# A decoder trunk: the order of its projections, its split buffers and the products of its recurrence

## The chip, the cores and the metric

The kernel runs on one core of one Trainium2 chip, as one program. The metric is the device time of one execution in microseconds (us). A profile of one execution stands beside it: it lists for each engine when it worked. PE (TensorE) multiplies matrices, PEld is its weight load, DVE (VectorE) and ACT (ScalarE) work element by element, POOL (GpSimd) does small and strided work, and SP (SyncE) issues most of the transfers. Each engine works through its own queue of instructions in order.

## The reference, cut to what matters

256 tokens of 2048 features pass through one layer of a hybrid decoder. The weights are read once, and all of it is float32.

```
h  = RMSNorm(x)
c, b, xa, za, q, f, iv, og, ga, gb = split(h @ W_in)
yA = b * conv3(c * xa) * silu(za)
o  = gated recurrence over the tokens: queries silu(q), keys (1-lb)*sigmoid(-f),
     values iv, decay lb + (1-lb)*sigmoid(f) per token and feature, 8 heads of 128
yB = RMSNorm per head(o) * silu(og)
x  = x + (sigmoid(ga) * (yA @ W_a) + sigmoid(gb) * (yB @ W_b)) @ W_o
x  = x + sigmoid(RMSNorm(x) @ W_pg) * (p @ W_pp)
out = RMSNorm(x)
```

The last but one line matters for the first two parts of the change: p @ W_pp (called PP here; p has only 256 features) depends on nothing before it, while RMSNorm(x) @ W_pg (called PG, the gate) needs all that comes before.

The recurrence matters for the third. For a pair of tokens s <= t of one head, its matrix is a[s, t] = sum over k of key[s, k] * query[t, k] * exp(B[t, k] - B[s, k]), where B is the running sum of the logarithm of the decay. A product of matrices can only be formed if the exponential is split into one factor for s and one for t, and for numbers that don't overflow both have to be taken from a reference token between s and t. So the matrix is cut by levels: at level B, the tokens are in blocks of B, and pairs that lie in the two halves of the same block take the middle of the block as reference. What is left (blocks of 2) is corrected by one factor per pair.

## The kernel before, in words

**Streaming.** The weights arrive as chunks of 256 rows by 512 columns. `load` (L94) issues the transfers into three raw buffers of two chunks each. `split` (L108) writes each chunk as a high part in fp32r on ScalarE (`whi`, L118) and the rest on VectorE (`wlo`, L119), into one of four pairs of buffers, or of six "late" pairs near the end. `product` (L844) multiplies it: three fp32r matmuls of 128x512 (L847 to L849) for each of two feature blocks and each of two halves of the tokens, so twelve a chunk. The other operands are split in the same way by `put` (`xh` at L196 on ScalarE, `xl` at L197 on VectorE).

**The order of groups.** A group is 512 columns of one weight matrix, in all its chunks (eight, four for W_a and W_b, one for W_pp). The list `groups` (L124) sets the order: the fields of W_in in two rounds (f, q, iv, og, c, xa, za, b, with j = 0 and then 1), then ga, gb, A and B four times, then O four times, then PP0, PG0, PP1, PG1, PP2, PG2, PP3, PG3. Splits run three chunks ahead of the products (`ahead`, L840). Around the last group they run up to five further ahead. A group fills two PSUM banks of the four with the tag "g"; four more with the tag "s" serve the recurrence.

**Epilogues.** What becomes of a finished group is a generator (`ep_f`, `ep_q`, ..., `ep_pp` at L646, `ep_pg` at L653). The main loop advances each active one by a step per chunk, and the step's instructions are ordered behind that chunk's split on ScalarE and VectorE. The compiler's scheduler may move matmuls of independent groups past each other on TensorE. `ep_pp` copies the two banks of PP to SBUF (L649); `ep_pg` takes the sigmoid from the banks of PG (L659), multiplies, adds to x and squares. `ep_o` adds to x, and then brings the result into the layout with features on the partitions by way of DRAM (`turned`, L223: four writes, a read, and a transposition at L238), and `put` makes x1's operands of it, which PG needs.

**The recurrence.** `hgrn` (L350) runs once for each half of the heads (j = 0, 1), as part of the epilogue of og. It has six levels (LEVELS, L31: 128, 64, 32, 16, 8, 4). For each, `level` (L402) subtracts the reference (L413 on VectorE, L414 on POOL) and takes exponentials on ScalarE (L415, L416); `combine` (L387) multiplies them with keys and queries, two quarters on VectorE and two on POOL (L396); `products` (L364) forms a full 128x128 matrix for each of four heads (L368); `keep` (L371) copies those entries that a mask names. A further burst of the same size is the block of the second 128 tokens against the first. Then the pairs of 2 are corrected by a factor and its reciprocal (L457 to L468), and one burst of eight products of 128x128 (L477) gives the diagonal blocks. The finished matrices meet the values at L488 to L490.

**Start and end.** The first transfers are x and the first chunk of f (L147 to L167, L723); eight bf16 matmuls without use keep TensorE busy until they land (L734). The last group is worked in three parts (L920), so that the end of the work behind it (`last_half`, L673, and `last_norm`, L688) is short.

The loop that issues all of this, with `steps` a flat list of (group, chunk):

```
for pos, (gi, c) in enumerate(steps[:last_group]):
    while done < min(pos + 1 + ahead(pos), len(steps)):
        split(done)
        done += 1
    product(psum[t], ...)
    advance()
    if c == nch - 1:
        active.append(epilogues[kind](j, psum))
        step(active[-1])
```

Of the kernel before, what the change touches and what calls it, by code (L numbers as in the profile page):

```python
# [15 lines left out]
P = 128  # L16
T = 256
# [13 lines left out]
LEVELS = [128, 64, 32, 16, 8, 4]  # L31
# [13 lines left out]
def hybrid_kernel(ctx, tc, xT, x, pT, prm, gfin, masks, w_in, w_a, w_b, w_o, w_pg, w_pp, out):  # L45
# [47 lines left out]

    def load(pos):  # L94
        w, g, c = stream[pos]
        nch = w.shape[2]
        key = (id(w), g, c // 2)
        if key not in loaded:
            raw = wp.tile([P, 2, 2 * CW], F32, tag="raw", bufs=3, name=nm("raw"))
            loaded[key] = raw  # L100
            if nch == 1 or FIRST <= pos < FIRST + 4:
                for i in range(min(nch, 2)):
                    nc.sync.dma_start(out=raw[:, i, :], in_=w[g, :, c + i, :])
            elif pos >= FIRST:
                nc.sync.dma_start(out=raw, in_=w[g, :, c : c + 2, :])
        return loaded[key]

    def split(pos, halves=(0, 1)):  # L108
        w, g, c = stream[pos]
        src = load(pos)[:, c % 2, :]  # L110
        pool, n = (pools["late"], 6) if pos >= last_group + 2 else (wp, 4)
# [12 lines left out]
    groups = []  # L124
# [15 lines left out]
    last_group = len(steps) - w_pg.shape[2]  # L140

    LEAD, AHEAD = 3, 4
    TOKENS, NORM = 6, 10
    FIRST = 6


    prm_t = const.tile([P, PRM_N], F32, name="prm_t")  # L147
    xraw = [t4() for _ in range(4)]
# [6 lines left out]
    def load_first(c, eng):  # L155

        raw, w = load(c)[:, c % 2, :], stream[c][0][0, :, c, :]
        for s in (slice(0, CW), slice(CW, 2 * CW)):
            eng.dma_start(out=raw[:, s], in_=w[:, s])


    load_first(0, nc.scalar)
    nc.sync.dma_start(out=prm_t, in_=prm)
    load_x(0, 1)
    load_x(1, 1)
    load_x(2, 2)
    load_first(1, nc.sync)  # L167
# [9 lines left out]
    carry = const.tile([P, 1024], F32, name="carry")  # L177
    nc.gpsimd.memset(carry, 1.0)
    nc.gpsimd.memset(carry.rearrange("p (n c) -> p n c", c=SCAN)[:, :, 0:1], 0.0)
    mask_t = const.tile([P, len(LEVELS) + 4, P], mybir.dt.int32, name="mask_t")  # L180
# [98 lines left out]
    def ep_f(j, psum):  # L279
# [16 lines left out]
        for h in range(4):  # L296
# [21 lines left out]
        nc.vector.tensor_tensor_scan(  # L318
            out=b, data0=carry, data1=lf, initial=0.0, op0=ALU.mult, op1=ALU.add
        )  # L320
# [29 lines left out]
    def hgrn(j):  # L350

# [8 lines left out]
        both = tmp.tile([P, 4, P], F32, tag="both", bufs=1, name=nm("both"))  # L360
        nc.gpsimd.memset(both, 0.0)
        aoff = tmp.tile([P, 4, P], F32, tag="aoff", bufs=1, name=nm("aoff"))

        def products(X):  # L364
            bk = bank("s")
            for h in range(4):
                s = slice(h * P, (h + 1) * P)
                nc.tensor.matmul(bk[:, s], X[:, 0, h, :], X[:, 1, h, :], start=True, stop=True)  # L368
            return bk

        def keep(dst, mask, src):  # L371
            nc.vector.copy_predicated(
                out=dst, mask=mask_t[:, mask : mask + 1, :].to_broadcast([P, 4, P]), data=src
            )
# [12 lines left out]
        def combine(e, B):  # L387

            X = t4("X", 2).rearrange("p (w h t) -> p w h t", w=2, h=4)
            ev, kv, qv = tiles(e, B), tiles(kT, B), tiles(qT, B)  # L390
            xv = X.rearrange("p w h (n two c) -> p w h n two c", two=2, c=B // 2)
            for w, blk, half, src, eng in (
                (0, 0, 0, kv, nc.vector), (0, 1, 1, kv, nc.gpsimd),
                (1, 1, 0, qv, nc.vector), (1, 0, 1, qv, nc.gpsimd),
            ):
                eng.tensor_tensor(  # L396
                    out=xv[:, w, :, :, half, :], in0=ev[:, :, blk, :, half, :], in1=src[:, :, blk, :, half, :],
                    op=ALU.mult,
                )
            return X  # L400

        def level(B):  # L402

            n, h = 1024 // B, B // 2
# [3 lines left out]
            if B > SCAN:  # L408
                nc.scalar.activation(out=el, in_=halves(y, B)[0], func=AF.Exp, scale=-1.0)
                nc.scalar.activation(out=er, in_=br, func=AF.Exp)  # L410
            else:
                ref = bl[:, :, h - 1 : h].to_broadcast([P, n, h])
                nc.vector.tensor_tensor(out=el, in0=bl, in1=ref, op=ALU.subtract)  # L413
# [3 lines left out]
            return combine(e, B)  # L417


# [6 lines left out]
        X = level(LEVELS[0])  # L426
        yield
        yield
        for i in range(len(LEVELS)):
            nxt = level(LEVELS[i + 1]) if i + 1 < len(LEVELS) else None  # L430
            bk = products(X)
            yield
            yield
            keep(both, i, heads(bk))
            yield
            X = nxt

# [9 lines left out]
        X = t4("X", 2).rearrange("p (w h t) -> p w h t", w=2, h=4)  # L447
        ev, kv, qv = (z.rearrange("p (h k t) -> p h k t", h=4, k=2) for z in (e, kT, qT))
        nc.vector.tensor_tensor(out=X[:, 0], in0=ev[:, :, 0], in1=kv[:, :, 0], op=ALU.mult)
        nc.gpsimd.tensor_tensor(out=X[:, 1], in0=ev[:, :, 1], in1=qv[:, :, 1], op=ALU.mult)  # L450

        f, rf = (t4()[:, :512] for _ in range(2))
        bl, br = halves(b, 2)
        nc.vector.tensor_tensor(
            out=f.rearrange("p (n c) -> p n c", c=1), in0=br, in1=bl, op=ALU.subtract
        )
        nc.scalar.activation(out=f, in_=f, func=AF.Exp)  # L457
        nc.vector.reciprocal(out=rf[:, :256], in_=f[:, :256])
        yield
        nc.vector.reciprocal(out=rf[:, 256:], in_=f[:, 256:])  # L460
        yield
        bo = products(X)
        k2, q2 = tiles(kT, 2), tiles(qT, 2)
        fv, rv = (z.rearrange("p (h k n) -> p h k n", h=4, k=2) for z in (f, rf))
        for blk in range(2):
            kk, qq = k2[:, :, blk, :, 1 - blk, 0], q2[:, :, blk, :, 1 - blk, 0]
            nc.vector.tensor_tensor(out=kk, in0=kk, in1=rv[:, :, blk], op=ALU.mult)
            nc.gpsimd.tensor_tensor(out=qq, in0=qq, in1=fv[:, :, blk], op=ALU.mult)  # L468
            keep(a[:, blk], len(LEVELS) + blk, both)
        yield  # L470
        nc.vector.tensor_copy(out=aoff.rearrange("p h t -> p (h t)"), in_=bo)
        yield
        bk = [bank("s") for _ in range(2)]
        for blk in range(2):
            for h in range(4):
                s = slice(h * T + blk * P, h * T + (blk + 1) * P)
                nc.tensor.matmul(  # L477
                    bk[blk][:, h * P : (h + 1) * P], kT[:, s], qT[:, s], start=True, stop=True
                )
        yield  # L480
        yield
        for blk in range(2):
            keep(a[:, blk], len(LEVELS) + 2 + blk, heads(bk[blk]))
        yield
        o = [bank("s") for _ in range(2)]
        for h in range(4):
# [5 lines left out]
            )  # L492
        yield
# [152 lines left out]
    def ep_pp(j, psum):  # L646
        pw = t4("pw", 2)
        for t in range(NT):
            nc.scalar.activation(out=pw[:, t * CW : (t + 1) * CW], in_=psum[t], func=AF.Copy)  # L649
        state["pw", j] = pw  # L650
        yield

# [360 lines left out]
```

## Time and profile before

| | |
|---|---|
| median of 3 runs | 842.39 us (842.17 to 842.98) |
| span of the profiled execution | 840.7 us, 9809 instructions |
| its own time beside the span | none is given; the runs are 1.5 to 2.3 us longer than the span |
| busy, of the span | PE 98%, DVE 63%, ACT 52%, POOL 11% |
| read from HBM, written | 170.82 MB, 11.53 MB, 217 GB/s over the span |

How to read what is quoted of the profile: a line of the time line has the start in us, the duration in us, the engine, the line of the kernel (L847), the operation, the tile that is written and those that are read (buffer numbers left out), and the shapes. "x4" means four of them in a row. "[3.67 <-ACT t L659]" means that the engine was idle for 3.67 us before, and that the instruction of L659 on ScalarE released it. A line of the groups has the busy time in us and the mean of one in ns, and behind the second bar the idle time before them with its releasers. A line of the chain has the start, the time on the chain, and what it was. Matmuls overlap: one is given as 0.39 us long, but the next one starts after less than that, so their price is the distance between starts. An fp32 product appears as two matmul records, an fp32r product as one.

### The profile page before, as it was taken

Reading aid. Unit: us, or ns where it says so; the run is one execution under the profiler, and the core shown is the slowest. Engines: PE = TensorE matmul, PEld = TensorE weight load, DVE = VectorE, ACT = ScalarE, POOL = GpSimd, SP = SyncE. Lnnn points to the kernel's source line nnn. Section 1 sums busy time; section 2 is a strip of 40 time slices with the busy share of each in tenths; the row PEclk is TensorE's granted clock in tenths of the full one; section 3 lists DMA queues with packets and bytes.
Section 4 is the critical chain, followed back from the end, with each engine's and each line's share of the span. In section 5 each row is a group of like instructions: output and inputs, shape, how many; then the busy total and the mean of one; then the engine's idle time right before and its main releaser. Section 6 shows DMA issues by size and latency. Waiting matters only on the chain.

```text
span 840.7 us, 9809 instructions
## 1 busy us (share of the span) xinstructions
PE 824.8 (98%) x3752; PEld 684.8 (81%) x3752; DVE 528.3 (63%) x600; ACT 435.9 (52%) x563; POOL 91.6 (11%) x76
## 2 busy tenths in 40 slices
PE   8999999999999999999999999999999999999985
PEld 6888888888888888888888888888888888878865
DVE  6557687777674777877546446455555666655552
ACT  7565654545564654545544444444444555654543
POOL 1000054100000243100001001001001000002110
PEclk9999999999999999999999999999999999999998
DMA  9976555648775555458557557556556877864522
GB/s 327 375 257 242 186 198 172 229 151 267 267 236 189 193 196 187 168 190 285 186 195 244 200 200 232 195 189 232 203 200 220 288 262 259 306 229 175 201 76 101
DMA packets 40080, 183.01 MB, mean 218 GB/s; under 512 B 4576, under 2 KB 14048, under 8 KB 22112
## 3 DMA queue, kind: packets, MB, share of 16 engines
q1 hardware_dynamic: 39456, 181.33, 62.2%
q10 hardware_dynamic: 576, 1.05, 0.4%
q8 instruction: 29, 0.48, 0.2%
q14 instruction: 19, 0.16, 0.1%
HBM read 170.82 MB, written 11.53 MB: 217 GB/s over the span
## 4 chain that ended last, share of the span: by engine, by line
PE 95%; DMA 2%; issue 1%; ACT 1%; DVE 1%; POOLq 0%; POOL 0%; SPq 0%; ACTq 0%
PE g L847 31%; PE g L849 31%; PE g L848 31%; PE s L368 1%; DMA raw<-in_w_pg 1%; DVE wlo L119 1%; ACT whi L118 1%; PE s L477 0%; DMA t<-in_xT 0%; PE s L490 0%; PE s L489 0%; PE s L488 0%; ACT xs L700 0%; ACT t L683 0%; DVE t L679 0%
## 5 line engine op out<-in xcount | busy, mean ns | idle before, releaser
L119 DVE TENSOR_TENSOR wlo<-raw,whi 128x1024 fp32r<-128x1024 f32 (+1 forms) x294 | 360.3, 1229 | 273.5 <-ACT whi L118 273.0
L118 ACT ACTIVATE whi<-raw 128x1024 fp32r<-128x1024 f32 (+1 forms) x294 | 309.0, 1053 | 353.4 <-PE g L849 316.1
L847 PE MATMUL g<-whi,xh 128*128 128x512 f32 (+1 forms) x912 | 353.6, 389 | 6.0 <-ACT t L659 3.7
L848 PE MATMUL g<-wlo,xh 128*128 128x512 f32 (+1 forms) x912 | 353.1, 387 | 0.0
L849 PE MATMUL g<-whi,xl 128*128 128x512 f32 (+1 forms) x912 | 352.6, 387 | 0.1
L847 PEld LDWEIGHTS g<-whi,xh 128*128 128x128 f32 x912 | 172.2, 189 | 41.6 <-ACT t L659 4.1
L849 PEld LDWEIGHTS g<-whi,xl 128*128 128x128 f32 x912 | 172.1, 189 | 35.1 <-DVE xl L197 0.5
L848 PEld LDWEIGHTS g<-wlo,xh 128*128 128x128 f32 x912 | 172.0, 189 | 34.3 <-DVE wlo L119 0.5
L848 PE MATMUL g<-wlo,mh 128*128 128x512 f32 x128 | 49.6, 389 | 0.0
L849 PE MATMUL g<-whi,ml 128*128 128x512 f32 x128 | 49.5, 389 | 0.0
L847 PE MATMUL g<-whi,mh 128*128 128x512 f32 x128 | 49.5, 389 | 0.0
L613 POOL TENSOR_TENSOR t<-ga,gb 128x512 f32<-128x512 f32 x8 | 14.1, 1791 | 249.1 <-DVE gb L609 249.1
L849 PEld LDWEIGHTS g<-whi,ml 128*128 128x128 f32 x128 | 24.0, 188 | 5.0
L848 PEld LDWEIGHTS g<-wlo,mh 128*128 128x128 f32 x128 | 24.0, 188 | 5.0
L847 PEld LDWEIGHTS g<-whi,mh 128*128 128x128 f32 x128 | 24.0, 188 | 4.9
L414 POOL TENSOR_TENSOR t<-b 128x512 f32<-128x512 f32 x10 | 20.9, 2086 | 65.3 <-DMA raw<-in_w_in 33.6
L396 POOL TENSOR_TENSOR X<-t,kT 128x256 f32<-128x256 f32 x12 | 14.1, 1174 | 99.4 <-ACT t L410 57.7
L847 PE MATMUL g<-whi,yaTh 128*128 128x512 f32 x64 | 24.9, 389 | 0.0
L848 PE MATMUL g<-wlo,yaTh 128*128 128x512 f32 x64 | 24.9, 389 | 0.0
L849 PE MATMUL g<-whi,yaTl 128*128 128x512 f32 x64 | 24.9, 389 | 0.0
L847 PE MATMUL g<-whi,ybTh 128*128 128x512 f32 x64 | 24.9, 389 | 0.0
L848 PE MATMUL g<-wlo,ybTh 128*128 128x512 f32 x64 | 24.9, 389 | 0.0
(148 smaller groups left out, 556.1 us busy)
## 6 DMA issues: line engine op xcount, KB each, us to landing
raw<-in_w_in SPq DMA_DIRECT2D x91, 1024.0 KB, 4.9
raw<-in_w_o SPq DMA_DIRECT2D x16, 1024.0 KB, 5.4
raw<-in_w_pg SPq DMA_DIRECT2D x16, 1024.0 KB, 4.8
turn<-t SPq DMA_DIRECT2D x72, 128.0 KB, 2.9
t<-turn SPq DMA_DIRECT2D x18, 512.0 KB, 5.1
raw<-in_w_a SPq DMA_DIRECT2D x8, 1024.0 KB, 5.0
raw<-in_w_b SPq DMA_DIRECT2D x8, 1024.0 KB, 5.0
raw<-in_w_in SPq DMA_DIRECT2D x8, 512.0 KB, 7.8
```

The lines of the kernel that those rows point to most:

```text
L118: a = nc.scalar.activation(out=hi[:, s], in_=src[:, s], func=AF.Copy)
L119: v = nc.vector.tensor_tensor(out=lo[:, s], in0=src[:, s], in1=hi[:, s].bitcast(F32), op=ALU.subtract)
L368: nc.tensor.matmul(bk[:, s], X[:, 0, h, :], X[:, 1, h, :], start=True, stop=True)
L396: eng.tensor_tensor(out=xv[:, w, :, :, half, :], in0=ev[:, :, blk, :, half, :], in1=src[:, :, blk, :, half, :], op=ALU.mult,)
L414: nc.gpsimd.tensor_tensor(out=er, in0=br, in1=ref, op=ALU.subtract)
L613: nc.gpsimd.tensor_tensor(out=spread(m, t), in0=blocks(ga[:, s]), in1=blocks(gb[:, s]), op=ALU.add)
L847: nc.tensor.matmul(psum, oh, hi, start=first, stop=False)
L848: nc.tensor.matmul(psum, oh, lo, start=False, stop=False)
L849: nc.tensor.matmul(psum, ol, hi, start=False, stop=last)
```

## The change

Three things are changed together.

1. **PP first.** The four PP groups move to the front of the list, ahead of f. p's two feature blocks and the chunks of W_pp are the first transfers. `ep_pp` copies each result to SBUF (one bank on ScalarE, one on VectorE, some chunks later) and writes it to a DRAM buffer, 512 KB for each; `load_pw` reads it back when the gate's group starts. PP2 and PP3 use the banks with the tag "s". O is followed by PG0, PG1, PG2, PG3 directly.
2. **Ten pairs for the gate.** From the gate's first chunk on (`gate`), four of ten chunks go to the four pairs of before and six to the "late" pairs, so that ten pairs serve all the gate's groups. `ahead` grows by one for every four chunks.
3. **The recurrence in blocks of 32.** The levels 32, 16, 8 and 4 only have entries inside the diagonal blocks of 32x32. For each head, level and block there is now one product of 32 rows by 32 columns (over all 128 features), whose place among the columns of TensorE is given by `tile_position`; the 64 of a half come as one burst. A second burst has the 32x32 blocks of level 64 (16), those of the final diagonal (32), the 64x64 blocks of level 128 (8) and the four full products of the second 128 tokens against the first. Masks shrink to 32 columns. The multiplies of `combine` are all on VectorE, the reference is subtracted from the whole tile on VectorE, and the reciprocal becomes exp(-x) with one Newton step. The scan over 1024 columns becomes four of 256.

The core of the diff (new lines have new numbers; L706 of the changed file is the copy of a PP bank on ScalarE, L901 to L903 are its large products):

```diff
-LEVELS = [128, 64, 32, 16, 8, 4]
+LEVELS = [32, 16, 8, 4]
+NARROW, Q = len(LEVELS), 32
...
+        pool, n = (pools["late"], 6) if pos >= gate and (pos - gate) % 10 >= 4 else (wp, 4)
...
+    groups = [("PP", j, w_pp, j, "pT") for j in range(4)]
...
-    for j in range(4):
-        groups.append(("PP", j, w_pp, j, "pT"))
-        groups.append(("PG", j, w_pg, j, "x1T"))
+    groups += [("PG", j, w_pg, j, "x1T") for j in range(4)]
...
+    gate = len(steps) - 4 * w_pg.shape[2]
...
+    load_half(0, 0, nc.scalar)
+    for k in range(2):
+        nc.sync.dma_start(out=praw[:, k * T : (k + 1) * T], in_=pT[:, k, :])
+    load_half(0, 1, nc.scalar)
+    for i in range(2):
+        load_half(1, i, nc.sync)
     nc.sync.dma_start(out=prm_t, in_=prm)
-    load_x(0, 1)
-    load_x(1, 1)
-    load_x(2, 2)
-    load_first(1, nc.sync)
+    for c in (2, 3):
+        for i in range(2):
+            load_half(c, i, nc.sync)
+    for c in (0, 1):
+        for i in range(2):
+            load_half(FIRST + c, i, nc.sync)
+        load_x(2 * c, 2)
+    load_x(4, 2)
+    load_x(6, 2)
...
-                ref = bl[:, :, h - 1 : h].to_broadcast([P, n, h])
-                nc.vector.tensor_tensor(out=el, in0=bl, in1=ref, op=ALU.subtract)
-                nc.gpsimd.tensor_tensor(out=er, in0=br, in1=ref, op=ALU.subtract)
+                n, h = 1024 // B, B // 2
+                ref = bl[:, :, h - 1 : h].to_broadcast([P, n, B])
+                nc.vector.tensor_tensor(
+                    out=e.rearrange("p (n c) -> p n c", c=B), in0=b.rearrange("p (n c) -> p n c", c=B),
+                    in1=ref, op=ALU.subtract,
+                )
...
+        def combine(e, B):
+            X = operands()
+            ev = tiles(e, B)
+            xv = X.rearrange("p w h (n two c) -> p w h n two c", two=2, c=B // 2)
+            for w, src in ((0, tiles(kT, B)), (1, tiles(qT, B))):
+                for half in range(2):
+                    blk = half if w == 0 else 1 - half
+                    nc.vector.tensor_tensor(
+                        out=xv[:, w, :, :, half, :], in0=ev[:, :, blk, :, half, :], in1=src[:, :, blk, :, half, :],
+                        op=ALU.mult,
+                    )
+            return X
+        def tile_product(out, X, h, n, i, m):
+            s, t = (slice(z * n, (z + 1) * n) for z in (i, m))
+            nc.tensor.matmul(out, X[:, 0, h, s], X[:, 1, h, t], start=True, stop=True, tile_position=(0, i * n))
...
+        for B in LEVELS:
+            e = decays(B)
             yield
+            Xs.append(combine(e, B))
...
+        small_b = bank("s")
+        small_v = small_b.rearrange("p (l h c) -> p l h c", l=NARROW, h=4)
+        for h in range(4):
+            for l in range(NARROW):
+                for i in range(4):
+                    tile_product(small_v[i * Q : (i + 1) * Q, l, h, :], Xs[l], h, Q, i, i)
...
+        nc.scalar.activation(out=near, in_=small_v[:, 0], func=AF.Copy)
+        for l in range(1, NARROW):
+            keep(
+                near, near_m[:, l : l + 1, :].to_broadcast([P, 4, Q]), small_v[:, l]
+            )
...
+        nc.vector.tensor_tensor(out=g, in0=f, in1=rf, op=ALU.mult)
+        yield
+        nc.vector.tensor_scalar(out=g, in0=g, scalar1=-1.0, scalar2=2.0, op0=ALU.mult, op1=ALU.add)
+        nc.vector.tensor_tensor(out=rf, in0=rf, in1=g, op=ALU.mult)
...
+        wide, diag, across = (bank("s") for _ in range(3))
+        w128 = wide[:, : 4 * 64].rearrange("p (h c) -> p h c", h=4)
+        w64 = wide[:, 4 * 64 : 4 * 96].rearrange("p (h c) -> p h c", h=4)
+        dv = diag[:, : 8 * Q].rearrange("p (k h c) -> p k h c", k=2, h=4)
+        for h in range(4):
+            for i in range(4):
+                tile_product(w64[i * Q : (i + 1) * Q, h, :], X64, h, Q, i, i ^ 1)
+            for blk in range(2):
+                for i in range(4):
+                    s = slice(h * T + blk * P + i * Q, h * T + blk * P + (i + 1) * Q)
+                    nc.tensor.matmul(
+                        dv[i * Q : (i + 1) * Q, blk, h, :], kT[:, s], qT[:, s], start=True, stop=True,
+                        tile_position=(0, i * Q),
+                    )
+        for h in range(4):
+            for i in range(2):
+                tile_product(w128[i * 64 : (i + 1) * 64, h, :], X128, h, 64, i, 1 - i)
+        for h in range(4):
+            s = slice(h * P, (h + 1) * P)
+            nc.tensor.matmul(across[:, s], Xo[:, 0, h, :], Xo[:, 1, h, :], start=True, stop=True)
...
-        pw = t4("pw", 2)
-        for t in range(NT):
-            nc.scalar.activation(out=pw[:, t * CW : (t + 1) * CW], in_=psum[t], func=AF.Copy)
-        state["pw", j] = pw
-        yield
+        pw = t4()
+        for _ in range(2):
+            yield
+        nc.scalar.activation(out=pw[:, :CW], in_=psum[0], func=AF.Copy)
+        yield
+        nc.vector.tensor_copy(out=pw[:, CW:], in_=psum[1])
+        yield
+        yield
+        nc.sync.dma_start(out=pw_d[:, j, :], in_=pw)
+    def load_pw(j):
+        state["pw", j] = t4("pw", 2)
+        nc.sync.dma_start(out=state["pw", j], in_=pw_d[:, j, :])
...
-        return LEAD + min(max(pos - (last_group - 8), 0), 5)
+        return LEAD + min(max(pos - gate, 0) // 4, 5)
...
+            nc.gpsimd.memset(full_m, 0)
+            for i in range(4):
+                z = slice(i * Q, (i + 1) * Q)
+                nc.sync.dma_start(out=near_m[z], in_=masks[z, :NARROW, z])
+                nc.sync.dma_start(out=full_m[z, :, z], in_=masks[z, NARROW:, z])
...
-            psum = [bank("g") for _ in range(NT)]
+            psum = [bank("s" if kind == "PP" and j >= 2 else "g") for _ in range(NT)]
```

More of the change, by code (lines that the diff above doesn't have):

```diff
@@ L359, in hgrn @@
         nc.gpsimd.memset(a, 0.0)
-        both = tmp.tile([P, 4, P], F32, tag="both", bufs=1, name=nm("both"))
-        nc.gpsimd.memset(both, 0.0)
+        near = tmp.tile([P, 4, Q], F32, tag="near", bufs=1, name=nm("near"))
         aoff = tmp.tile([P, 4, P], F32, tag="aoff", bufs=1, name=nm("aoff"))
[L364 to L374, printed above, removed]
         def heads(ap):
```

201 lines of the change are left out of this document (104 added, 97 removed).

## The prediction, made before the result was known

> **What bounds the kernel now.** I read the page's first, second and fourth parts, then the groups of TensorE by shape, then the time lines around each idle stretch that these groups name.
>
> ```profile
> span 840.7 us, 9809 instructions
> PE 824.8 (98%) x3752; PEld 684.8 (81%) x3752; DVE 528.3 (63%) x600; ACT 435.9 (52%) x563; POOL 91.6 (11%) x76
> ...
> PE   8999999999999999999999999999999999999985
> ...
> PE 95%; DMA 2%; issue 1%; ACT 1%; DVE 1%; POOLq 0%; POOL 0%; SPq 0%; ACTq 0%
> ```
>
> TensorE bounds every stage: busy 98% of the span, 95% of the chain that ended last, low only at both ends. So an edit counts only if it takes time out of TensorE's queue or puts time in. Other engines matter where TensorE waits for them, which the groups by shape list:
>
> ```profile
> L847 PE MATMUL g<-whi,xh 128*128 128x512 f32 x880 | 344.6, 393 | 6.0 <-ACT t L659 3.7 <-ACT xh L196 1.5 <-ACT whi L118 0.8
> ...
> L368 PE MATMUL s<-X 128*128 128x128 f32 x112 | 14.7, 274 | 0.0
> ...
> L477 PE MATMUL s<-qT,kT 128*128 128x128 f32 x32 | 3.9, 275 | 0.0
> ```
>
> Three waits in all, 3.7, 1.5 and 0.8 us. The busy time of a matmul overlaps its neighbours', so prices come from start to start. The first two waits, in the time line:
>
> ```profile
> 744.86 0.39 PE L847 MATMUL g<-whi,ph 128*128 128x512 f32 x1
> ...
> 747.35 0.39 PE L849 MATMUL g<-whi,pl 128*128 128x512 f32 x1
> 747.78 1.06 ACT L118 ACTIVATE whi<-raw 128x1024 fp32r<-128x1024 f32 x1 [1.66 <-PE g L849]
> 748.74 1.69 ACT L196 ACTIVATE xh<-t,prm_t 128x256 fp32r<-128x256 f32 x4
> ...
> 749.28 0.50 PE L847 MATMUL g<-whi,xh 128*128 128x512 f32 x1 [1.54 <-ACT xh L196]
> ...
> 750.54 0.73 PE L849 MATMUL g<-whi,xl 128*128 128x512 f32 x2
> 751.11 0.39 PE L847 MATMUL g<-whi,xh 128*128 128x512 f32 x1
> ```
>
> PP1's twelve matmuls run from 744.86 to 747.35: 2.49 us over 11 steps, 0.227 a step. From 747.35 to 751.11 there are seven steps, worth 1.59 us, in 3.76: **2.2 us lost**, because the gate's group PG0 has reached O3's features, whose xh (L196) and xl (L197) aren't there.
>
> ```profile
> 803.92 0.39 PE L849 MATMUL g<-whi,pl 128*128 128x512 f32 x1
> 806.30 1.06 ACT L118 ACTIVATE whi<-raw 128x1024 fp32r<-128x1024 f32 x1 [3.41 <-DMA raw<-in_w_pg]
> 807.27 1.25 ACT L659 ACTIVATE t<-g,r2r 128x512 f32<-128x512 f32 x2
> ...
> 807.99 0.55 PE L847 MATMUL g<-whi,xh 128*128 128x512 f32 x1 [3.67 <-ACT t L659]
> 808.34 0.63 PE L848 MATMUL g<-wlo,xh 128*128 128x512 f32 x1
> ...
> 811.74 0.39 PE L847 MATMUL g<-whi,xh 128*128 128x512 f32 x1
> ```
>
> From 803.92 to 811.74 there are ten steps, worth 2.27 us, in 7.82: **5.55 us lost**. The last group needs a PSUM bank that PG2's sigmoid (L659) must empty; it stands on ScalarE behind a split (L118) that waited 3.41 us for its raw weights. After 3.67 us idle, the steps are 0.43 us up to 811.74, half the clock: some 1.9 of the 5.55.
>
> **The change part by part.** The large products stay the same in number, so I add up only what differs.
>
> *End gaps.* In the changed program the PP groups no longer stand between the gate's groups. The ring of four banks then gives the last group a bank that PG1 used, not PG2, and PG1's was emptied while PG2 ran (8 chunks x 12 steps x 0.227 = 21.8 us earlier); and ten split pairs let splits run ahead of their products. The wait at 807.99 has no cause left: −5.55. For the gap at 749, the order of the changed program puts 34 matmuls of PG1 (34 x 0.227 = 7.7 us) between PG0's sixth and seventh chunk, in place of PP1's 12 (2.7) and after PP0's 12 are gone (2.7). Seen from O3's end, PG0's last chunks start at 6 x 2.72 + 7.7 = 24.0 us; today 747.35 + 0.23 stands at 2.72 + 16.3 + 2.72 = 21.8, and xh comes 1.7 later, at 23.5. Even with today's lag xh is in time and xl at most 0.5 late; without PP0's splits and copies it is earlier. I take −2.2 (end: −1.7). What is late next at this place is the tail after the last product, which isn't touched.
>
> *Start.*
>
> ```profile
> 0.74 0.38 SPq L163 DMA_DIRECT2D prm_t<-in_prm  x1
> ...
> 1.18 1.37 SPq L151 DMA_DIRECT2D t<-in_xT  x3
> ...
> 4.74 0.51 ACT L196 ACTIVATE xh<-t,prm_t 128x256 fp32r<-128x256 f32 x1 [1.58 <-DMA t<-in_xT]
> ...
> 5.82 1.22 PE L847 MATMUL g<-whi,xh 128*128 128x512 f32 x2 [0.77 <-ACT whi L118]
> ```
>
> The first operand is now half of p, of the same 128x256, issued first on SP's queue instead of second, 0.44 us sooner. The chain behind it (xh, whi, product) is the same: −0.4 (ends 0 and −0.4). The four PP groups need no x, so x and f's weights have 10 us more to land.
>
> *A new wait.* f's first product (group f0, after PP3) takes a bank of PP0, which ScalarE empties at the changed file's L706. In ScalarE's order this copy stands behind the split of f's fourth chunk and four xh. That split needs a pair that PP3's last product frees, as only four pairs serve this stage. The same train stands in the rows around 747: a matmul starts at 747.35, the split it releases at 747.78, the xh at 748.74 (1.69 for four, to 750.43). Then the copy, priced by today's:
>
> ```profile
> L649 ACT ACTIVATE pw<-g 128x512 f32<-128x512 f32 x8 | 4.4, 587 | 0.0
> ```
>
> That ends at 751.02, and TensorE starts some 0.05 later: 3.72 after the last matmul's start, less its own step of 0.227: **+3.5 us**. Queued behind the copy are f0's later splits, which TensorE needs only three chunks on. It is certain in place, since order and pairs fix it; open is the clock afterwards. Above, 3.67 us idle was followed by half clock (+1.9) and 1.54 wasn't. Here the idle is some 3.35 by the profile's count; I take the full clock as likeliest, narrowly, and hold the other as a rival.
>
> *The recurrence on TensorE.* Per half (two halves), six level bursts and one off-block burst of 8 records, and one of 16:
>
> ```profile
> 105.90 0.89 PE s L368 x8
> ...
> 172.09 1.78 PE s L477 x16
> ```
>
> So 7 x 0.89 + 1.78 = 8.0 us leave, at 0.111 a record of 128 columns. In come 64 + 48 products of 32x32, two records each: 224 narrow records; 16 records of 64 columns; 8 of 128 (0.89). No row has a narrow one. Two rows tell how time goes with columns:
>
> ```profile
> 825.76 0.28 PE L848 MATMUL g<-wlo,xh 128*128 128x256 f32 x1
> ...
> 830.80 0.28 PE L848 MATMUL g<-wlo,xh 128*128 128x256 f32 x1
> ```
>
> These are 42 steps of 256 columns in 5.04 us, 0.120 each; 512 columns take 0.227, so 256 columns cost 0.107 and the rest is fixed. A record of 128 fp32 columns at 0.111 then looks like two passes of 128 (0.107) and 0.0045 fixed. A 32-column record: 0.0267 + 0.0045 = **0.031 us**; 64 columns: 0.058. Per half 224 x 0.031 + 16 x 0.058 + 0.89 = 8.8, for both halves **+1.5 us**. Each further 10 ns per narrow record is 448 x 0.01 = 4.5 us. Ends: below, products in four column groups side by side, a quarter, 0.008: −8.8 from +1.5 less what waits give back; above, no saving with width, 0.111: +35.8 on top. I take 0.031, since both slopes fit columns.
>
> The Trainium skill, "TensorEngine Tiling (Array Packing)", section "Key Properties", says that changing the tiling mode drains TensorE; a drain here would be at most the 0.16 by which a matmul's 0.39 exceeds its step, and ten changes then 1.6 us. No row has such a change; today's bursts enter and leave at no extra, and I add nothing.
>
> *Other engines there.* The level multiplies leave POOL for VectorE, and five subtractions a half grow from half to whole tiles:
>
> ```profile
> 105.00:190.00 85.00, 85.00 (x424) 72.12 (x424) 66.49 (x84) 42.92 (x63) 26.01 (x19) 1.00 0.54 186
> ...
> L413 DVE TENSOR_TENSOR t<-b 128x512 f32<-128x512 f32 x10 | 12.4, 1245 | 0.0
> L396 DVE TENSOR_TENSOR X<-t,kT 128x256 f32<-128x256 f32 x12 | 12.8, 1070 | 1.8 <-ACT t L409 1.8
> L396 DVE TENSOR_TENSOR X<-t,qT 128x256 f32<-128x256 f32 x12 | 6.0, 503 | 0.0
> L458 DVE RECIPROCAL t<-t 128x256 f32<-128x256 f32 x2 | 3.5, 1748 | 0.0
> ```
>
> The window's third engine column is VectorE: 66.49 of 85. Per half it loses 5 x 1.245 + 6 x 1.070 + 6 x 0.503, two reciprocals (3.4) and some 10 of merging; it gains 5 subtractions of 1.22, 24 multiplies (about 0.46 when POOL is quiet), a Newton step (1.9) and some 8 of merging: about the same sum in fewer, denser chunks. Scheduled by hand from these rows, the first burst's last operand is ready some 2 us ahead of TensorE, and the second's (kT scaled by the Newton step) about when TensorE gets there: 0 (end: +4 a half). The p projections' way through DRAM, 2 MB each way, and eight mask loads in place of one lie beside a queue with slack: 0.
>
> *Sum.* 840.7 − 5.55 − 2.2 − 0.4 + 3.5 + 1.5 = 837.6 for the span. The page's execution has no time of its own beside its span; the median of the runs, 842.39, lies 1.7 above it, and I add that: **839.3 us**, 0.37% faster.
>
> **The rivals.**
>
> *Half clock after the f0 wait.* Everything as above, but the 3.35 us of idle bring 0.43-us steps for nine matmuls, as after 807.99: 841.2. For: the nearest row is that 3.67. Against: it is the only one, and the idle here is shorter. The Trainium skill, "TensorE: Matmul & The Clock Gate", section "Why this matters for your kernels", warns of idle gaps over about 3 us between bursts; by that rule this rival holds.
>
> *Narrow products cost a fixed price.* The place is the two bursts of each half; the weight load and product of each record come with a price that doesn't shrink with width. At half of today's record, 0.056, both halves pay 448 x 0.025 = +11.2: 850.5, slower. It decides from 0.031 + 3.1/448 = 0.038 on, where the gain is used up. For: each product brings its own load, and no row shows a pair under 0.111. Against: both wide shapes show only 5 to 14 ns fixed. At the far end, 0.111, it is 875. The Trainium skill, "TensorE: Matmul & The Clock Gate", section "Wait — 56ns, not 53.3ns?", gives a floor of about 25 ns between starts, or about 62 ns per matmul where decode goes through microcode; by 25 the sum stays, by 62 it is 853, slower; no row here shows either.
>
> *Side by side.* The four column groups of a block run together: 0.008 to 0.015 a record, −7 to −10, of which up to 1.8 a half goes back as waits for kT: 829 to 834. For: the products name different column groups. Against: nothing in the trace overlaps matmuls beyond their 0.16 us of latency.
>
> *VectorE late.* Its denser stretch (24 multiplies with short inner runs) makes TensorE wait 1 to 4 us a half: 841 to 847. For: it was busy 66.49 of 85 us with POOL's help. Against: its own sum doesn't grow.
>
> **How the numbers follow.** Forecast 0.26; half clock 0.17; fixed price 0.27, the far end 0.06; side by side 0.16; VectorE late 0.08. About 0.2%, 1.7 us, is what a measurement of this kernel can tell from no change, so faster is below 840.7 and slower above 844.1. Faster: 0.25 of the forecast, 0.03 of half clock, 0.16 side by side: 0.44. Same: 0.01 + 0.14 + 0.04 of VectorE late: 0.19. Slower: 0.27 + 0.06 + 0.04: 0.37. The forecast with its clock alone spans 837.5 to 842. The range takes in side by side to 830 and a fixed price to 0.064 a record, 854; the far end and side by side's tip stay out.
>
> **What would show it.** No idle before the last group nor at PG0's end (each step by its own row); one idle of about 3.4 us near 18 us, released by L706; the bursts' length, first burst 128 records: 4.0 us at 0.031, 7.2 at 0.056, 1 to 2 side by side. A first burst above 5 us, or waits of TensorE for VectorE between 40 and 380 us, makes the forecast wrong.

## The result, and the profile after

The changed kernel takes **831.12 us** (830.94 to 831.21, 4 runs) against 842.68 (842.17 to 843.15, 4 runs): a ratio of 0.9864, 95% interval 0.985 to 0.9878. It is 1.4% faster, where 0.4% was forecast (839.3). The time lies in the range, near its lower end, which was there for a rival; the likeliest case had the size of the gain wrong by a factor of almost four.

The page of the changed kernel, and its groups of TensorE by shape (busy us, mean ns, idle before and its releaser):

```profile
span 829.4 us, 10481 instructions
PE 815.1 (98%) x4104; PEld 674.4 (81%) x4104; DVE 520.8 (63%) x634; ACT 438.2 (53%) x577; POOL 35.6 (4%) x35
```

```profile
L901 PE MATMUL g<-whi,xh 128*128 128x512 f32 x880 | 343.6, 391 | 3.6 <-ACT t L706 3.6
...
L902 PE MATMUL g<-wlo,pop 128*128 128x512 f32 x8 | 3.5, 434 | 0.8 <-DVE wlo L124 0.8
...
L425 PE MATMUL s<-X 128*32 128x32 f32 x320 | 4.4, 199 | 0.0
...
L517 PE MATMUL s<-qT,kT 128*32 128x32 f32 x128 | 1.9, 198 | 0.0
L425 PE MATMUL s<-X 128*64 128x64 f32 x32 | 1.4, 228 | 0.0
```

TensorE is as full as before (98%) and has 352 more matmul records, yet is busy for 9.7 us less. Of its three waits for operands, those of 3.7 and 1.5 us at the end are gone; a new one of 3.6 us, released by L706, is the forecast wait of f's first product. The narrow records (32 columns) have a mean of 199 ns, but most of it overlaps with their neighbours; what they cost shows in the time line around the first burst of a half, and then around the second:

```profile
139.80 0.39 PE L903 MATMUL g<-whi,xl 128*128 128x512 f32 x1
140.12 1.30 PE L425 MATMUL s<-X 128*32 128x32 f32 x128
141.34 0.50 PE L901 MATMUL g<-whi,xh 128*128 128x512 f32 x1
...
160.31 0.39 PE L903 MATMUL g<-whi,xl 128*128 128x512 f32 x1
...
162.20 1.16 PE L526 MATMUL s<-X 128*128 128x128 f32 x8
163.12 0.48 PE L901 MATMUL g<-whi,xh 128*128 128x512 f32 x1
```

All 128 records end within 1.30 us of the first one's start. Less the 0.20 of the last one's own length that is 1.10 us for 127 steps, 0.0087 each, under a third of the 0.031 in the forecast. From the large product ahead of a burst to the one behind it, less one step of 0.227, the first burst takes 1.3 us and the second 2.6. The other deviation stands around the new wait:

```profile
17.28 0.39 PE L903 MATMUL s<-whi,pop 128*128 128x512 f32 x1
...
18.12 1.06 ACT L123 ACTIVATE whi<-raw 128x1024 fp32r<-128x1024 f32 x1 [0.18 <-DMA raw<-in_w_in]
...
19.09 1.69 ACT L215 ACTIVATE xh<-t,prm_t 128x256 fp32r<-128x256 f32 x4
...
20.68 1.05 ACT L706 ACTIVATE t<-g 128x512 f32<-128x512 f32 x2
21.31 0.50 PE L901 MATMUL g<-whi,xh 128*128 128x512 f32 x1 [3.64 <-ACT t L706]
...
25.29 0.39 PE L902 MATMUL g<-wlo,xh 128*128 128x512 f32 x1
```

From 17.28 to 21.31 is 4.03 us, less one step of 0.227: 3.8 lost. The ten steps from 21.31 to 25.29 take 3.98 where 2.27 would do: the half clock costs 1.7 more.

The account of the span, each term from the two time lines (us):

| term | forecast | measured | from |
|---|---|---|---|
| the two gaps at the end | −7.75 | −7.7 | no idle of TensorE there any more |
| start | −0.4 | −1.1 | first product at 4.82 (before 5.82), and 1.8 lost after it up to 17.28 (before 1.9 up to 16.4) |
| wait of f's first product | +3.5 | +5.5 | 3.8 and 1.7 of half clock |
| recurrence on TensorE | +1.5 | −7.9 | its bursts and the late start of the matmul behind each: 21.5 before, 13.6 after; 5.4 of both are the products with the values, which are the same |
| sum | −3.1 | −11.2 | spans: 840.7 to 829.4, −11.3 |

### The profile page after: what moved, and what is told of

The parts are those of the page before. It is cut to its first block, busy times and chain, and to the rows that moved or that the text cites. A ratio compares the mean times of both kernels' runs of the same rounds, so it can differ in the third digit from the quotient of the medians.

```text
span 829.4 us, 10481 instructions
## 1 busy us (share of the span) xinstructions
PE 815.1 (98%) x4104; PEld 674.4 (81%) x4104; DVE 520.8 (63%) x634; ACT 438.2 (53%) x577; POOL 35.6 (4%) x35
## 4 chain that ended last, share of the span: by engine, by line
PE 95%; DMA 2%; issue 1%; ACT 1%; DVE 0%; SPq 0%; POOLq 0%; POOL 0%; ACTq 0%
PE g L901 31%; PE g L903 31%; PE g L902 31%; DMA raw<-in_w_in 1%; DMA raw<-in_w_pp 1%; PE s L425 1%; PE s L526 0%; PE s L545 0%; PE s L544 0%; PE s L543 0%; ACT xh L215 0%; ACT xs L764 0%; PE s L517 0%; ACT whi L123 0%; ACT t L747 0%
## 5 line engine op out<-in xcount | busy, mean ns | idle before, releaser
L901 PE MATMUL g<-whi,xh 128*128 128x512 f32 (+1 forms) x912 | 352.6, 387 | 3.6 <-ACT t L706 3.6
L903 PE MATMUL g<-whi,xl 128*128 128x512 f32 (+1 forms) x912 | 352.4, 387 | 0.0
L901 PEld LDWEIGHTS g<-whi,xh 128*128 128x128 f32 x912 | 171.8, 188 | 38.4 <-ACT t L706 4.1
L903 PEld LDWEIGHTS g<-whi,xl 128*128 128x128 f32 x912 | 171.7, 188 | 34.5
L901 PE MATMUL g<-whi,mh 128*128 128x512 f32 x128 | 49.5, 389 | 0.0
L903 PE MATMUL g<-whi,ml 128*128 128x512 f32 x128 | 49.5, 389 | 0.0
L901 PEld LDWEIGHTS g<-whi,mh 128*128 128x128 f32 x128 | 24.0, 188 | 5.0
L903 PEld LDWEIGHTS g<-whi,ml 128*128 128x128 f32 x128 | 24.0, 188 | 5.0
L903 PE MATMUL g<-whi,yaTl 128*128 128x512 f32 x64 | 24.9, 389 | 0.0
L901 PE MATMUL g<-whi,yaTh 128*128 128x512 f32 x64 | 24.9, 389 | 0.0
L903 PE MATMUL g<-whi,ybTl 128*128 128x512 f32 x64 | 24.9, 389 | 0.0
L901 PE MATMUL g<-whi,ybTh 128*128 128x512 f32 x64 | 24.9, 389 | 0.0
L257 DVE STREAM_TRANSPOSE t<-t 128x1024 f32<-128x1024 f32 x16 | 19.9, 1241 | 1.8 <-DMA t<-turn 1.8
```

Source lines behind the costliest of these rows:

```text
L257: nc.vector.transpose(out=dst.rearrange("p (k a e) -> p a k e", a=4, e=32), in_=src.rearrange("p (a k e) -> p a k e", a=4, e=32))
L901: nc.tensor.matmul(psum, oh, hi, start=first, stop=False)
L903: nc.tensor.matmul(psum, ol, hi, start=False, stop=last)
```

## The experiments

The theory formed from this account: the four terms are separate, and **narrow products whose neighbours name other column groups run side by side**, so that a record costs 0.0087 us instead of some 0.03. A column group is here the quarter (or half) of TensorE's columns that `tile_position` names. The rivals: a narrow record is cheap in any order; or the order of the weight groups gave more than the account says. Times are medians of 4 to 10 runs.

**1. One column group in a row.** In both bursts, the loop over the column groups `i` goes outermost; of the edit, the first burst:

```diff
-        for h in range(4):
-            for l in range(NARROW):
-                for i in range(4):
+        for i in range(4):
+            for h in range(4):
+                for l in range(NARROW):
                     tile_product(small_v[i * Q : (i + 1) * Q, l, h, :], Xs[l], h, Q, i, i)
```

> The changed kernel with the narrow products of both bursts in another order: all of one column group in a row, then the next group, so that neighbours share their columns of TensorE. Theory (products in different column groups run side by side, 0.010 us a record): in a row they fall back to 0.031 us a record, the first burst goes from 1.3 to 4.0 us, the 96 narrow records of the second from 1.0 to 3.0, its 64-column ones from 0.6 to 0.9; about +5 us a half, 841 us. Rival (a narrow record is cheap in any order): no change, 831. Second rival (a fixed price hidden only by the change of column group, 0.056): 849.

Measured: 841.61 us (840.66 to 842.86, 10 runs). The same 128 records, with the same shapes and data, in the time line of this kernel:

```profile
140.45 3.94 PE L425 MATMUL s<-X 128*32 128x32 f32 x128
```

(3.94 − 0.20) / 127 = 0.0295 a step, against 0.031 in the forecast. Only the order differs, so it is the change of column group that makes a record cheap. Both rivals fall, the record that is cheap in any order (831) and the price of 0.056 (849). In the trace's single starts, records of the same group are 0.031 to 0.032 apart, and 0.006 where the group changes. In the second burst that is so whether neighbours read the same tile (two products of kT) or different ones, so a shared operand isn't the cause. The place among the columns also fixes the 32 partitions of PSUM that are written; the runs don't separate these two. The two bursts of a half now take 8.9 us by the same count as in the table, where the forecast had 8.8.

**2. Two column groups in turn.** In both bursts, first groups 0 and 1 alternate, then 2 and 3; of the edit, the first burst:

```diff
-        for h in range(4):
-            for l in range(NARROW):
-                for i in range(4):
+        for z in range(2):
+            for h, l, i in ((h, l, i) for h in range(4) for l in range(NARROW) for i in (2 * z, 2 * z + 1)):
                     tile_product(small_v[i * Q : (i + 1) * Q, l, h, :], Xs[l], h, Q, i, i)
```

> The changed kernel with the narrow products ordered so that two column groups alternate, first groups 0 and 1, then 2 and 3. Theory (as many run side by side as there are different groups in a row): 0.015 us a narrow record, the first burst 1.9 to 2.0 us against 1.3 with four groups and 3.9 with one, the whole about 2.4 us longer than the changed kernel, 833.5. Rival (any change of group hides the price, however many there are): 831.1.

Measured: 834.04 us (833.83 to 835.21), and

```profile
140.08 2.12 PE L425 MATMUL s<-X 128*32 128x32 f32 x128
```

(2.12 − 0.20) / 127 = 0.0151, half of the price of one group. So the price is that of one record divided by the number of groups in turn: 0.0295, 0.0151, and with four 0.0087. The single starts say it more exactly: one round through the groups takes 0.032 us, whether it has one, two or four of them; the start of a burst and the changes of group account for the rest of these means.

**3. Wide weights for the same narrow products.** In the first burst the weights are all 128 columns of keys, and 32 columns of queries are streamed. The four blocks of a head and level overwrite each other, so this kernel leaves out the recurrence's near pairs:

```diff
-                    tile_product(small_v[i * Q : (i + 1) * Q, l, h, :], Xs[l], h, Q, i, i)
+                    nc.tensor.matmul(
+                        small_v[:, l, h, :], Xs[l][:, 0, h, :], Xs[l][:, 1, h, i * Q : (i + 1) * Q],
+                        start=True, stop=True,
+                    )
```

> The changed kernel with the first burst's 64 products taken with all 128 columns of keys as the weights and 32 columns of queries streamed, without a place among the columns; the blocks of one head and level overwrite each other, so this part of the recurrence's matrix is wrong. Theory (the time of a record is that of the larger of its two sides, weight columns or streamed columns): the load of 128 columns sets it, 0.107 to 0.111 us a record, the burst takes 14 instead of 1.3 us, 856 to 857 us. Rival (only streamed columns count): 0.031 a record, 4.0 us a burst, 836.5. Second rival (a record is cheap whatever its shape): 831.

Measured: 879.72 us. The first line below is of the time line at the burst's start, the others are of two windows inside it (the column behind POOL is the granted clock):

```profile
140.89 1.31 PE L465 MATMUL s<-X 128*128 128x32 f32 x11
```

```profile
142.54:145.94 3.40, 3.40 (x32) 3.40 (x32) 2.36 (x2) 0.99 (x2) 0.00 (x0) 1.00 0.64 267
145.96:159.00 13.04, 13.04 (x64) 13.04 (x63) 0.46 (x2) 0.13 (x1) 0.00 (x0) 0.50 0.00 0
```

The first eleven records step by (1.31 − 0.27) / 10 = 0.104 us, near the theory's 0.107 to 0.111: a quarter of the streamed columns saves almost nothing when the weights stay 128 wide. The 23 us beyond the expectation are the clock, which no theory here had. TensorE is busy in every microsecond of both windows, but from 145.95 on it is granted half the clock, and 64 records take 13 us, 0.204 each. Half clock lasts 20.5 us here, up to 166.43, and 27.3 at the other half's burst; at half speed these lose about 24.

**4. The recurrence of before in the new order, and 5. the new recurrence in the old order.** `hgrn` and its masks are exchanged as a whole between the two kernels (4 keeps the four scans). In 4, with the reverse in 5:

```diff
-LEVELS = [32, 16, 8, 4]
-NARROW, Q = len(LEVELS), 32
+LEVELS = [128, 64, 32, 16, 8, 4]
...
-    near_m = const.tile([P, NARROW, Q], mybir.dt.int32, name="near_m")
-    full_m = const.tile([P, 4, P], mybir.dt.int32, name="full_m")
+    mask_t = const.tile([P, len(LEVELS) + 4, P], mybir.dt.int32, name="mask_t")
```

> The changed order of groups and the ten pairs, with the recurrence of the kernel before. Theory (separate terms: end gaps -7.75, start -1.0, wait for the PP bank +5.5, recurrence -8.1): 842.7 - 7.75 - 1.0 + 5.5 = 839.4 us. Rival (the order gives most of the gain, the recurrence little): 831 to 834.

> The kernel before with the new recurrence alone. Theory (separate terms): 842.7 - 8.1 = 834.6 us, with both end gaps as they were. Rival (the recurrence gives little alone): 841 or more, for instance because VectorE now makes TensorE wait in the kernel before's tighter start of the splits.

Measured: 839.67 us (839.07 to 840.39) for the order alone and 836.94 (835.39 to 837.87) for the recurrence alone. The first is as the account has it (839.4). The second is 2.3 longer than expected. Its group of large products, beside the same line quoted of before:

```profile
L886 PE MATMUL g<-whi,xh 128*128 128x512 f32 x880 | 344.2, 392 | 7.8 <-ACT t L698 5.2 <-ACT xh L198 1.5 <-ACT whi L119 1.1
```

The wait before the last group is 5.2 us here instead of 3.7, and the start 0.3 longer (1.1 for 0.8): 1.8 of the 2.3. The split ahead of the sigmoid that ends that wait itself waits for a transfer, so its length isn't a constant, as the sum of terms took it; the bursts themselves are as short as in the changed kernel. The other 0.5 stands behind the last matmul: from its start to the end of the span there are 9.3 us here (826.06 to 835.3) and 8.7 before (832.00 to 840.7), where the output is written.

**6. Only the bank of the last group.** The kernel before, with one word changed:

```diff
-        bk, n = bank("g"), CW // 2
+        bk, n = bank("s"), CW // 2
```

> The kernel before, with the last group's banks taken from the recurrence's four (tag s), which are free by then, and nothing else changed. Theory (the wait before the last group is for its PSUM bank alone): that wait and the half clock after it go, 5.5 us less, 837.1. Rival (the splits, which wait for raw weights at the same time, hold the last group anyway): 0 to 2 us less, 840.6 to 842.6.

Measured: 836.73 us (836.39 to 837.23), 5.4 less than before, and no idle at that place:

```profile
803.75 0.39 PE L849 MATMUL g<-whi,pl 128*128 128x512 f32 x1
803.98 0.39 PE L847 MATMUL s<-whi,xh 128*128 128x512 f32 x1
```

The PSUM bank alone was the wait; the splits, which wait for raw weights at the same place before, don't hold the last group here.

**7. The changed kernel with four pairs.** `split` and `ahead` are those of before:

```diff
-        pool, n = (pools["late"], 6) if pos >= gate and (pos - gate) % 10 >= 4 else (wp, 4)
+        pool, n = (pools["late"], 6) if pos >= last_group + 2 else (wp, 4)
```

> The changed kernel with the split pairs of before: four pairs up to the last group, the six late ones only for it. Theory A (the two end gaps went because the p projections no longer stand between the gate's groups, so the banks turn over later; the ten pairs only pay for PG0's end): the wait before the last group stays away, but PG0's last chunks come before O3's features are in place: TensorE idles some 2 to 5 us near PG0's end, 833 to 836 us. Theory B (the ten pairs are what removes the wait before the last group): both gaps back, 837 to 840. Rival (neither needs the ten pairs): 831.

Measured: 831.17 us (829.45 to 831.4), and neither gap in the groups:

```profile
L901 PE MATMUL g<-whi,xh 128*128 128x512 f32 x880 | 343.2, 391 | 3.4 <-ACT t L706 3.4
```

The rival is right: the ten pairs buy nothing. The scheduler puts the same 34 matmuls of PG1 ahead of PG0's last two chunks with four pairs.

**8. The copies earlier.** `ep_pp` copies without waiting two steps, and the split of f's fourth chunk and the features of its fourth to sixth are queued behind the copies:

```diff
-        for _ in range(2):
-            yield
-        nc.scalar.activation(out=pw[:, :CW], in_=psum[0], func=AF.Copy)
+        copy = nc.scalar.activation(out=pw[:, :CW], in_=psum[0], func=AF.Copy)
+        state.setdefault("copies", []).append(copy.ins)
...
+                    for ins in state["copies"][:2] if done == 7 else ():
+                        behind.enter_context(tc.issue_after(ins))
```

> The changed kernel with the copies of the PP banks put ahead of the split of f's fourth chunk on ScalarE. Theory (f's first product waits only for that copy, 3.6 us, and the half clock after it costs another 1.7): no idle near 18 us, full clock, 5.5 us less, 825.6 us. Rival (f's own operands are as late as the copy): the wait stays at over 1.5 us with another releaser, 828 to 831.

Measured: 827.68 us (827.45 to 827.81), 3.4 less than the changed kernel instead of 5.5. The half clock is gone, but two short waits are left:

```profile
16.99 1.06 ACT L123 ACTIVATE whi<-raw 128x1024 fp32r<-128x1024 f32 x1 [0.66 <-DMA raw<-in_w_in]
...
17.95 1.07 ACT L704 ACTIVATE t<-g 128x512 f32<-128x512 f32 x2
18.58 0.50 PE L900 MATMUL g<-whi,xh 128*128 128x512 f32 x1 [0.89 <-ACT t L704]
...
19.22 1.28 DVE L707 COPY t<-g 128x512 f32<-128x512 f32 x2
...
19.96 0.50 PE L900 MATMUL g<-whi,xh 128*128 128x512 f32 x1 [0.41 <-DVE t L707]
```

The releaser is still the copy: it stands behind the third chunk's split, which waits for its raw weights, and VectorE's copy of the second bank behind that split's low part. f's own operands were not late.

**9. The copies behind the fourth chunk's split, ahead of the four xh.** The same edit, with `done in (8, 9)` for the features alone:

> The changed kernel with the copies of the PP banks behind the split of f's fourth chunk but ahead of the four xh. Theory (idle over some 3 us brings the half clock, less doesn't): the wait before f's first product shrinks by the xh's 1.7 to some 2 us and the clock stays full: 831.1 - 1.7 - 1.7 = 827.7. Rival (any idle of 2 us brings it): 829.4.

Measured: 830.34 us (828.88 to 830.65). The expectation fails in the clock:

```profile
17.56 0.39 PE L902 MATMUL s<-whi,pop 128*128 128x512 f32 x1
19.95 0.50 PE L900 MATMUL g<-whi,xh 128*128 128x512 f32 x1 [1.99 <-ACT t L704]
...
21.37 0.79 PE L900 MATMUL g<-whi,xh 128*128 128x512 f32 x1 [0.46 <-DVE t L707]
...
23.24 0.63 PE L901 MATMUL g<-wlo,xh 128*128 128x512 f32 x1
```

After 1.99 and 0.46 us of idle, with three matmuls between them, the steps are 0.43 up to 24.50. A single idle of over 3 us isn't needed; what is, the last section works out.

**10. More warming in the kernel before.** `WARM = 10` in place of 8.

> The kernel before with ten idle bf16 matmuls at the start in place of eight, so that TensorE is busy up to its first real product (5.9 us). Theory (the 0.8 us of idle between the warming matmuls and the first product keeps the clock at half up to 9.7 us): full clock from the first product or soon after, some 1.7 us less, 840.9. Rival (the step to full clock comes at a time that has nothing to do with this idle): no change within 0.3, 842.6.

Measured: 843.32 us (840.3 to 845.3, 10 runs), ratio to before 1.0002 (0.9987 to 1.0017). The steps at the start are indeed at full clock (0.227 to 0.24 from 6.91 on), but at the recurrence's first burst the kernel is 0.07 us ahead (105.83 for 105.90): waits for x and weights take the place of the slow steps. And the clock fell elsewhere, after an idle that the kernel before has too without that:

```profile
749.21 0.50 PE L847 MATMUL g<-whi,xh 128*128 128x512 f32 x1 [1.54 <-ACT xh L196]
...
751.12 0.63 PE L847 MATMUL g<-whi,xh 128*128 128x512 f32 x1
...
754.11 0.51 PE L848 MATMUL g<-wlo,xh 128*128 128x512 f32 x1
```

**11. The copies of PP0 and PP1 on both engines behind f's second chunk.** As in 8, with `done in (6, 7, 8, 9)` for the features, `done in (6, 7)` for the splits, and VectorE's copies in the list too.

> The changed kernel with the copies of PP0's and PP1's banks, on ScalarE and VectorE, put right behind the split of f's second chunk, ahead of the transfer that the split of its third chunk waits for. Theory (the rest of 1.8 us that the earlier copy left were a split waiting for its raw weights ahead of the ScalarE copy, and the VectorE copy behind a split's low part): no idle at f's first product at all, 5.5 us less than the changed kernel: 825.6. Rival (x or f's weights land too late as well): 827 to 828.

Measured: **825.68 us** (825.57 to 825.73), ratio to before 0.9792 (0.9773 to 0.9812). This is faster than both kernels. f follows PP3 without a step lost:

```profile
17.25 0.39 PE L903 MATMUL s<-whi,pop 128*128 128x512 f32 x1
17.48 0.39 PE L901 MATMUL g<-whi,xh 128*128 128x512 f32 x1
```

## Why the prediction was wrong, point by point

**The step that failed** is "The recurrence on TensorE": "A 32-column record: 0.0267 + 0.0045 = 0.031 us", taken "since both slopes fit columns". As the price of one record alone it is right to 5% (0.0295 with one group in a row). It failed where it multiplied this price by the number of records. `tile_position` puts neighbours in different column groups, and these overlap: 0.0151 with two groups, 0.0087 with four. Without the products with the values, the bursts that leave were right (16.0 forecast, 16.1 measured), and those that come take 8.2 in place of 17.5. So the term is −7.9 and not +1.5: 9.4 us below the forecast. f's wait and the clock after it (+2.0) and the start (−0.7) leave the 8.2 between 839.3 and 831.1, to 0.1. The rival "side by side" had the mechanism, the time (829 to 834) and the length of the first burst (1 to 2 us, measured 1.3), and was given 0.16, because nothing in the trace of before overlaps matmuls beyond their latency. But every product of that trace has weights of 128 columns (128*128 in each group), so its silence was no evidence. The changed kernel names a place among the columns in every narrow product; that was the line to weigh.

**Side by side's price for VectorE** ("up to 1.8 a half goes back as waits for kT") did not appear: no matmul of the recurrence waits (idle 0.0 in its groups above). "VectorE late" falls with it; in the window of the first half VectorE is busy 65.33 us of 85, before 66.49:

```profile
105.00:190.00 85.00, 85.00 (x619) 70.80 (x618) 65.33 (x95) 52.37 (x80) 0.96 (x1) 1.00 0.55 185
```

**"Narrow products cost a fixed price"** falls with experiment 1: even in a row, a record of 32 columns takes 0.03 and not 0.056 or 0.111. Its argument that each product brings its own load was half right: with weights of 128 columns a record takes 0.104 us however little is streamed (experiment 3), but not with weights of 32.

**Two rules that were weighed.** The Trainium skill, "TensorE: Matmul & The Clock Gate", section "Wait — 56ns, not 53.3ns?", has starts never closer than about 25 ns. For one column group the trace agrees (0.0295 a record); with groups in turn records start 0.0087 apart, so here the measurement decides. The drain at changes of the tiling mode (the Trainium skill, "TensorEngine Tiling (Array Packing)", section "Key Properties") is small: the first narrow record starts 0.32 us after the matmul ahead of it, where a step is 0.227, so at most 0.1 at that change.

**The end gaps** were right, place and size (−7.7). The reason given for the last one, the bank, is shown alone by experiment 6. The ten pairs were given a part in it that they don't have (experiment 7). That PG1's 34 matmuls close the gap at PG0's end fits experiment 7, which keeps them and has no gap; no run takes them away alone.

**The wait of f's first product** was right in its chain, row by row, and 0.3 short in its length (3.8): the split began 0.84 after the last matmul (17.28 to 18.12) instead of 0.43, 0.18 of it for its raw weights. The clock was the wrong choice of two: +1.7. Neither choice had the reason (last section).

**The start** was mis-sized (−1.1 for −0.4): the first operand's split starts, p's half having landed, at 3.83, where x's did at 4.74. That the loss behind the first product stayed (1.9 to 1.8) is luck: before, it is eight steps at half clock up to 9.40; here it is mostly waits for split weights, the longest 0.76.

## What to carry to other kernels

A small product costs its full time only while its neighbour wants the same columns of TensorE. Order products that fill a quarter of the columns so that four different quarters come in turn, and price them at the record's time divided by the number of quarters. Narrow the weights too: with 128 columns of weights a record took 0.104 us for 32 streamed columns and 0.111 for 128. A PSUM bank is an operand: look for the copy that empties it and for what stands ahead of that copy in its engine's queue; a bank that was freed late cost 5.4 us in two places here.

## What the runs showed of the hardware that was not expected

The granted clock doesn't follow the length of one idle stretch. Half clock came after idle of 3.67 (before), 3.64 (after), 1.99 and 0.46 (experiment 9) and 1.54 with a few tenths behind it (experiment 10); it didn't come after the same 1.54 in the kernel before, nor after 0.89 and 0.41 (experiment 8).

The traces show what equal stretches differ in. The granted clock changes only at times that are whole multiples of 3.41 us apart: half clock lasts from 808.29 to 811.71 before, from 21.86 to 25.27 after, and for 6 and 8 such steps in experiment 3. The full clock between them lasts whole multiples too (798.72 us, 234 steps, before and after). Counting whole steps back from such a change gives the grid of a trace. How full TensorE was in one step goes with the clock of the next:

| kernel | step (us) | TensorE busy in it | clock in the next step |
|---|---|---|---|
| before | 746.85 to 750.27 | 0.55 | full |
| before | 804.88 to 808.29 | 0.09 | half |
| after | 15.04 to 18.45 | 0.77 | full |
| after | 18.45 to 21.86 | 0.16 | half |
| experiment 8 | 15.28 to 18.70 | 0.74 | full |
| experiment 9 | 17.64 to 21.06 | 0.37 | half |
| experiment 10 | 747.51 to 750.92 | 0.53 | half |

So the same idle can cost something or nothing by where it falls on this grid, and the grid lies elsewhere in each execution. The border isn't sharp in this count, in which the ends of matmuls are modelled: 0.53 and 0.55 differ, and one step at the very end of experiment 6 (824.90 to 828.32, busy 0.48) is followed by full clock. What the clock counts stays open. It is not the profile's busy time: in experiment 3 TensorE is busy all through the step from 142.54 to 145.95, and half clock follows. There each record streams 32 columns in 0.104 us; by the prediction's slope they take 0.027, an estimate of a quarter of the time. So a burst that is bound by its loads halved its own speed, and that of the products behind it up to 166.43.
